# q and k of a fused encoder layer stored as high and low parts by their projections; stores of rows and memory tiles from GpSimd's queue; the memory tokens' splits issued step by step

## The chip, the cores and the metric

The kernel runs on one core of a Trainium2 chip. Its time is the device time of one execution in microseconds; three runs of the kernel before took 1416.4, 1417.2 and 1421.53 us, the median is 1417.2 us. PE is the matrix engine, DVE (VectorE), ACT (ScalarE) and POOL (GpSimd) are the other three that compute, SP only issues transfers. Transfers can also be issued from GpSimd's instruction stream.

## The reference

One layer of a streaming encoder: 1024 tokens, 1024 channels, one batch, all in float32.

```python
h = rms_norm(x, mix_pre_g);  proj = h @ w_in          # 512 + 3*512 + 8 columns: u | q | k | v | f_logit
y_ssm = s5_mixer(u, ...)                              # 32 groups x 16 channels, 64 complex states, then GLU
y_fox = forgetting_attention(q, k, v, f_logit + b)    # 8 heads x 64, causal, bias cum[q] - cum[k]
x = x + rms_norm(concat(rms_norm(y_ssm), rms_norm(y_fox)) @ w_out)
h = rms_norm(x, xa_pre_g)
x = x + rms_norm(memory_cross_attention(h, rms_norm(mem), wq, wkv, wo))   # 4 heads, 256 memory tokens
h = rms_norm(x, ffn_pre_g)
x = x + rms_norm((silu(h @ w_gate) * (h @ w_up)) @ w_down)                # 2816 hidden columns
```

## The kernel before

**Splits.** Matmuls keep float32 accuracy by splitting operands: `split` (lines 113 to 120) lets ScalarE write a rounded high part (L114) and VectorE the low part, the difference (L116, or L118 where a gain is multiplied in). `mm3` (L123 to L125) then makes three products: high by high, high by low, low by high. `load_w` (L153 on) loads a weight tile of 512 KB (L159) into one of two buffers "raw", or into another buffer when `stage` is given, and splits it into one of three "whl" buffers.

**Buffers.** Tiles come from small pools and a new tile waits until the last use of the one before it in its buffer: "a" and "b" have 2 buffers of 4 KB per partition, "c" 3, "d" and "e" 1, "t2" (rows and small tiles that go out) 3, "slab" 16. PSUM has 4 banks "g" and two pairs "s" for scores.

**Order.** A scheduler of the language orders each engine's instructions by the order of the code and by priorities; `high_priority` raises one, `issue_after` (in `behind`) keeps instructions behind a named one. Each engine and each transfer queue then works in that order, and an instruction that waits holds up all behind it.

**The stages.** Up to about 222 us: the input projection. It makes u, then the tiles 4 to 7 of qk (k of two heads each), v's first half, the forget gate, the tiles 0 to 3 (q), and between these, by a fixed pace, the steps of `ssm` on VectorE (L616 to L619 and others; ACT L621 writes their result; SP L627 loads the tables T). `qk_tile` (L285) has PE work (`proj_tile`), one scaled evacuation by VectorE per half (L289) and one store of the tile to `qk_d` in DRAM, from GpSimd's queue (L293). Then `ssm_out` (L638, L639 on PE) together with v's second half. From 222 to about 480 us: forgetting attention, `fox`, head by head and query tile by query tile (64 steps). In each step PE makes the scores (L734, L735, the mask L737); VectorE adds the bias and finds the row's minimum of the negated scores (L741); ScalarE takes the exponential and its sum (L743); VectorE normalises (L748), or GpSimd for the tiles 1, 3 and 5 of the heads from 2 on (L746); two steps later PE transposes (L765), and L768 or L770 evacuates; every second step of an odd head PE multiplies by v (L779). `prepare` loads the next head's q and k by eight transfers of 128 KB, in two halves (L714, L715), and splits them: ScalarE the high parts (L718, L114), VectorE for heads 0 and 1 and GpSimd from head 2 on the low parts (L719, L116).

**The fillers.** Beside the attention, `paced` takes a step of the generator `fillers` per attention step: `glu`, the first rows of `out_ssm`, `mem_load` (the memory tokens multiplied by their norm, L967, and split, eight pieces), 16 times `mem_tile` (24 matmuls of 256 columns, the evacuation L979, the store to `kv_d` L980), the rest of `out_ssm` (evacuation L845, store to `t_d` L849, 16 of them), and the start of cross-attention. These stores go out on `stB`, which is SP's queue, as all the loads do. From 480 us on come the output projection (w_out_f, L1034), cross-attention and the feed-forward layer, which takes more than half of the time; no line of these is changed.

Of the kernel before, what the change touches and what calls it, by code (L numbers as in the profile page):

```python
# [34 lines left out]
MAGIC = 12582912.0  # L35
POOL_T = (1, 3, 5)
RATE = 1.02
# [16 lines left out]
def layer(ctx: ExitStack, tc: tile.TileContext, a, out):  # L54
# [94 lines left out]
    boost = 5000  # L149
    stA, stB, stC = pool, sp, pool  # L150

# [26 lines left out]

    qk_d = dram.tile([8, P, S], F32, name="qk_d")
    v_d = dram.tile([NT, P, 512], F32, name="v_d")  # L180
# [104 lines left out]
    def qk_tile(i, xH, xL, rb, ahead=False):  # L285
        o = tt("a")

        def evac(h, hs, ps):
            dve.scalar_tensor_tensor(out=by_chunk(o)[:, 4 * h:4 * h + 4], in0=ps.rearrange("p (j c) -> p j c", j=4),  # L289
                                     scalar=-0.125 if i < 4 else 1.0,  # L290
                                     in1=rb[0][:, hs].rearrange("p (j c) -> p j c", j=4), op0=ALU.mult, op1=ALU.mult)
        yield from proj_tile(load_w(a["w_f"][i], P), xH, xL, evac, ahead)
        stA.dma_start(out=qk_d[i], in_=o)  # L293

# [400 lines left out]


    def fox(yf):
        heads, units, pts = {}, {}, {}
        sv = const.tile([P, NT], F32, name="sv_f")

        def prepare(h):
            r0 = (h % 2) * 64
            qs = tt("a", [P, S], F32R)
            ka = slab([P, 2, S])
            ncb = tt("b")
            sp.dma_start(out=ncb, in_=nc_d[h:h + 1, :].broadcast_to([P, S]))
            heads[h] = (qs, ka, ncb)
            eng = dve if h < 2 else pool
            for hf in range(2):
                hs = slice(hf * 512, hf * 512 + 512)  # L710
                qk = tt("d" if h == 0 and hf else "e", [P, 2, 512])
                qd, kd = qk[:, 0], qk[:, 1]
                for rr in (0, 64):
                    sp.dma_start(out=qd[rr:rr + 64], in_=qk_d[h // 2, r0:r0 + 64, hs])  # L714
                    sp.dma_start(out=kd[rr:rr + 64], in_=qk_d[4 + h // 2, r0:r0 + 64, hs])  # L715
                yield
                with behind():
                    act.activation(out=qs[:, hs], in_=qd, func=AF.Copy)  # L718
                    eng.tensor_tensor(out=qs[64:128, hs], in0=qd[64:128], in1=qs[64:128, hs].bitcast(F32),  # L719
                                      op=ALU.subtract)  # L720
                    split(ka[:, 0, hs], ka[:, 1, hs], kd, lo_eng=eng)

        def behind():
            return tc.issue_after(last[-1].ins) if last else ExitStack()

        def scores(h, t):
            qs, ka, ncb = heads[h]
            ke = (t + 1) * P
            ps = s_ps([P, S])
            qt = qs[:, t * P:(t + 1) * P]  # L730
            for c0 in range(0, ke, 512):
                c1 = min(ke, c0 + 512)
                dg = c1 == ke
                pe.matmul(ps[:, c0:c1], qt, ka[:, 0, c0:c1], start=True, stop=False)  # L734
                pe.matmul(ps[:, c0:c1], qt, ka[:, 1, c0:c1], start=False, stop=not dg)  # L735
                if dg:
                    pe.matmul(ps[:, ke - P:ke], identb, maskb, start=False, stop=True)  # L737
            sc = tt("c")
            nlr = sm(3, "nlr")
            nm, l, rl = (nlr[:, i:i + 1] for i in range(3))  # L740
            dve.tensor_tensor_reduce(out=sc[:, :ke], in0=ps[:, :ke], in1=ncb[:, :ke], scale=1.0,  # L741
                                     scalar=3e38, op0=ALU.add, op1=ALU.min, accum_out=nm)
            last.append(act.activation(out=sc[:, :ke], in_=sc[:, :ke], func=AF.Exp, scale=-1.0, bias=nm, accum_out=l))  # L743
            dve.reciprocal(out=rl, in_=l)
            if t in POOL_T and h > 1:
                pool.tensor_tensor(out=sc[:, :ke], in0=sc[:, :ke], in1=rl.broadcast_to([P, ke]), op=ALU.mult)  # L746
            else:
                dve.tensor_scalar(out=sc[:, :ke], in0=sc[:, :ke], scalar1=rl, scalar2=None, op0=ALU.mult)  # L748
            units[h, t] = sc
# [53 lines left out]
        vs = {}  # L803
        drain(prepare(0))
        load_v(0)
        for n in range(-lag, len(seq) + 1):
            if n + lag < len(seq):
                h, t = seq[n + lag]
                scores(h, t)
                if t == 1 and h + 1 < NH:  # L810
                    nxt = prepare(h + 1)
                if t % 2 and h + 1 < NH:
                    step(nxt)
                if (h, t) == (3, 5):
# [12 lines left out]
    def out_ssm(ys):  # L827
        for cc in range(4):
            wh, wl = load_w(a["w_out_s"][cc], 256)
            for j0 in range(0, NT, 2):  # L830
# [128 lines left out]
    def mem_load(r, out):  # L959
# [3 lines left out]
        for k in range(0, KT, 4):  # L963
            m = raw([P, 4, 256])
            sp.dma_start(out=m, in_=a["memT"].rearrange("(k p) m -> p k m", p=P)[:, k:k + 4])
            for kk in range(4):
                dve.tensor_tensor(out=m[:, kk], in0=m[:, kk], in1=rb, op=ALU.mult)  # L967
                split(mh[:, k + kk], ml[:, k + kk], m[:, kk], g_mem[:, k + kk:k + kk + 1])
                if kk % 2:
                    yield  # L970
        out.extend((mh, ml))

    def mem_tile(i, mh, ml):
        wh, wl = load_w(a["wkv"][i], P)
        ps = g_ps([P, 256])
# [648 lines left out]
```

## Time and profile before

| what | value |
| --- | --- |
| median of three runs | 1417.2 us |
| lowest, highest run | 1416.4, 1421.53 us |
| the profiled execution's own time | 1418.95 us |
| its span in the profile | 1417.2 us |
| its mean granted clock of PE | 0.99 |
| transfers, mean rate | 163 GB/s |

The span is counted from the first to the last instruction. A row of a timeline gives start, duration, engine, line, operation, what it writes and reads, and in brackets the idle time of the engine before it with what ended it. "SPq" is SP's transfer queue; a row there gives when a transfer was issued, not when it landed. In a table of waits, the engine and line that waited come first, then the one that ended the wait. The granted clock is the share of full speed that the matrix engine was given.

### The profile page before, as it was taken

What the parts mean: (1) busy time and instruction counts of PE and PEld (TensorE: products, weight loads), DVE (VectorE), ACT (ScalarE), POOL (GpSimd) and SP (SyncE); (2) the same over time, 40 slices, a digit from 0 to 9 for tenths busy, and PEclk for the clock granted to TensorE, in tenths of its full rate; (3) what the DMA queues carried; (4) which work ended last, traced back from release to release, by engine and by line L of the source; (5) the groups of instructions that cost most, each with busy time, mean ns of one, the idle gap of its engine ahead of it and who ended that gap; (6) DMA issues with size and microseconds to landing.
All of it is one profiled execution on the core that took longest, in us unless ns stands there. A gap on an engine that the chain in (4) does not pass through costs nothing.

```text
span 1417.2 us, 20364 instructions
## 1 busy us (share of the span) xinstructions
PE 1382.1 (98%) x7353; PEld 1162.5 (82%) x7353; DVE 948.5 (67%) x1693; ACT 658.7 (46%) x1305; POOL 403.2 (28%) x424
## 2 busy tenths in 40 slices
PE   9999999899899898999999999999999999999997
PEld 7889898689789686888888888888888888888886
DVE  8939937946566677636457677777776676555566
ACT  7372347866566555434334533333333334544441
POOL 0001000113243134002021467676666661000021
PEclk9999999899999999999999999999999999999999
DMA  6225554246543756024457255554444546955544
GB/s 216 91 90 136 156 179 130 75 148 188 182 129 103 198 178 220 15 75 148 164 179 266 98 186 186 185 186 149 149 156 156 171 149 234 346 207 191 180 163 164
DMA packets 109366, 231.07 MB, mean 163 GB/s; under 512 B 11720, under 2 KB 46536, under 8 KB 109136
## 3 DMA queue, kind: packets, MB, share of 16 engines
q1 hardware_dynamic: 94064, 178.34, 39.4%
q0 software_dynamic: 15200, 51.42, 10.2%
q8 instruction: 58, 0.95, 0.3%
q14 instruction: 44, 0.36, 0.1%
HBM read 165.23 MB, written 73.14 MB: 168 GB/s over the span
## 4 chain that ended last, share of the span: by engine, by line
PE 59%; DVE 1%; ACT 0%; issue 0%; DVEq 0%; ACTq 0%
PE x L1289 17%; PE g L1289 13%; PE x L1552 7%; PE g L1552 7%; PE x L125 2%; PE x L124 2%; PE x L123 2%; PE g L123 2%; PE g L125 2%; PE g L124 2%; PE g L1074 1%; PE g L1185 1%; DVE slab L116 0%; DVE whl L116 0%; DVE c L1062 0%
## 5 line engine op out<-in xcount | busy, mean ns | idle before, releaser
L1289 PE MATMUL x<-slab,op 128*128 128x512 f32 x984 | 233.2, 389 | 0.5 <-DVE op L116 0.5
L1289 PEld LDWEIGHTS x<-slab,op 128*128 128x128 f32 x984 | 184.6, 188 | 39.3 <-DVE op L116 1.0
L1289 PE MATMUL g<-slab,op 128*128 128x512 f32 x744 | 178.7, 389 | 0.0
L116 DVE TENSOR_TENSOR slab<-slab 128x1024 fp32r<-128x1024 f32 (+2 forms) x92 | 110.3, 1207 | 86.7 <-ACT slab L114 84.8
L1289 PEld LDWEIGHTS g<-slab,op 128*128 128x128 f32 x744 | 139.6, 188 | 29.0
L123 PE MATMUL g<-slab,whl 128*128 128x512 f32 (+1 forms) x416 | 151.7, 365 | 1.1 <-ACT t L979 0.7
L125 PE MATMUL g<-slab,whl 128*128 128x512 f32 (+1 forms) x416 | 148.7, 358 | 0.0
L124 PE MATMUL g<-slab,whl 128*128 128x512 f32 (+1 forms) x416 | 148.4, 357 | 0.0
L114 ACT ACTIVATE slab<-slab 128x1024 fp32r<-128x1024 f32 (+2 forms) x92 | 94.9, 1037 | 106.3 <-DMA slab<-hs_d 82.7
L1552 PE MATMUL g<-slab 128*128 128x512 f32 x462 | 126.6, 389 | 0.0
L1552 PE MATMUL x<-slab 128*128 128x512 f32 x462 | 126.6, 389 | 0.0
L1552 PEld LDWEIGHTS x<-slab 128*128 128x128 f32 x462 | 86.7, 188 | 18.0
L1552 PEld LDWEIGHTS g<-slab 128*128 128x128 f32 x462 | 86.7, 188 | 18.0
L116 DVE TENSOR_TENSOR whl<-raw,whl 128x1024 fp32r<-128x1024 f32 (+2 forms) x61 | 71.1, 1168 | 36.7 <-ACT whl L114 36.5
L116 DVE TENSOR_TENSOR op<-slab,op 128x512 fp32r<-128x512 f32 x80 | 86.4, 1091 | 11.6 <-ACT op L114 11.4
L123 PE MATMUL g<-whl,slab 128*128 128x256 f32 (+2 forms) x288 | 86.1, 307 | 5.0 <-ACT t L845 3.4
L123 PEld LDWEIGHTS g<-slab,whl 128*128 128x128 f32 x416 | 78.6, 189 | 12.2 <-ACT t L979 0.9
L125 PEld LDWEIGHTS g<-slab,whl 128*128 128x128 f32 x416 | 78.4, 189 | 11.8 <-DVE whl L116 0.2
L1365 POOL TENSOR_TENSOR wt<-wt 128x256 f32<-128x256 f32 x88 | 81.8, 930 | 19.6 <-DMA wt<-in_w_down 16.1
L124 PEld LDWEIGHTS g<-slab,whl 128*128 128x128 f32 x416 | 78.6, 189 | 10.6
L114 ACT ACTIVATE op<-slab 128x512 fp32r<-128x512 f32 x80 | 50.0, 627 | 78.5 <-PE x L1289 36.8
L124 PE MATMUL g<-whl,slab 128*128 128x256 f32 (+2 forms) x288 | 85.7, 298 | 0.0
(389 smaller groups left out, 2930.7 us busy)
## 6 DMA issues: line engine op xcount, KB each, us to landing
hs_d<-ev POOLq DMA_DIRECT2D x77, 256.0 KB, 2.6
slab<-hs_d SPq DMA_DIRECT2D x35, 512.0 KB
wt<-in_w_down SPq DMA_DIRECT2D x44, 256.0 KB
wt_d<-wt POOLq DMA_DIRECT2D x22, 512.0 KB, 4.7
slab<-in_w_gate SPq DMA_DIRECT2D x20, 512.0 KB
slab<-in_w_up SPq DMA_DIRECT2D x20, 512.0 KB
slab<-wt_d SPq DMA_DIRECT2D x20, 512.0 KB
wd_d<-in_w_down SPq DMA_DIRECT2D x33, 256.0 KB
```

The lines of the kernel that those rows point to most:

```text
L114: first = act.activation(out=hi, in_=src, func=AF.Copy, scale=1.0 if mul is None else mul)
L116: (lo_eng or dve).tensor_tensor(out=lo, in0=src, in1=hi.bitcast(F32), op=ALU.subtract)
L123: pe.matmul(ps, lh, rh, start=first, stop=False)
L124: pe.matmul(ps, lh, rl, start=False, stop=False)
L125: pe.matmul(ps, ll, rh, start=False, stop=last)
L1074: pe.transpose(tp[:, k], src[:, (k0 + k) * P:(k0 + k + 1) * P], ident)
L1185: turned = pe.transpose(tp[:, k], h3[:, (4 * n + k) * P:(4 * n + k + 1) * P], ident)
L1289: pe.matmul(ps, x[:, k], y[:, k], start=first and k + n == 0, stop=k == 3 and n == 2, skip_group_check=not first)
L1365: pool.tensor_tensor(out=o, in0=x, in1=y, op=ALU.subtract)
L1552: pe.matmul(banks[n][j], xo[:, u, js], wo[:, v], start=ends[0] and k == 0, stop=ends[1] and k == 2, skip_group_check=onto is not None)
```

## The change

1. `qk_d` gets a second plane. `qk_tile` splits each half of its tile as soon as that is evacuated (the high part into a "t2" tile, the low part in place) and stores the high halves and then the low tile from GpSimd's queue. The input projection has 16 splits of 128x512 more, and 24 stores instead of 8.
2. `prepare` loads q (high parts in the first 64 partitions, low parts in the others) and k (both parts, twice) straight into the tiles that PE reads: four transfers of 256 or 512 KB instead of eight of 128 KB. No engine splits a head any more: ScalarE loses 32 operations, VectorE and GpSimd the subtractions beside them.
3. All normalisations are VectorE's (18 leave GpSimd).
4. `stB` is GpSimd's queue: the 32 stores of rows and memory tiles leave SP's.
5. In `mem_load`, multiply and split of a piece are issued behind the latest exponential.
6. Every third memory tile's weights, and the third set of w_out_s, are loaded into the "e" buffer, which the heads no longer use.

```diff
-POOL_T = (1, 3, 5)
-    stA, stB, stC = pool, sp, pool
+    stA, stB, stC = pool, pool, pool
-    qk_d = dram.tile([8, P, S], F32, name="qk_d")
+    qk_d = dram.tile([8, 2, P, S], F32, name="qk_d")
 def qk_tile(i, xH, xL, rb, ahead=False):
-        o = tt("a")
+        hl = tt("a", [P, S], F32R)
+        o = hl.bitcast(F32)
...
-        stA.dma_start(out=qk_d[i], in_=o)
+        for h in range(2):
+            hs = slice(h * 512, h * 512 + 512)
+            hi = t2t([P, 512], F32R)
+            split(hi, hl[:, hs], o[:, hs])
+            stA.dma_start(out=qk_d[i, 0, :, hs], in_=hi.bitcast(F32))
+        stA.dma_start(out=qk_d[i, 1], in_=o)
 def prepare(h):
-            eng = dve if h < 2 else pool
-            for hf in range(2):
...
-                    sp.dma_start(out=qd[rr:rr + 64], in_=qk_d[h // 2, r0:r0 + 64, hs])
-                    sp.dma_start(out=kd[rr:rr + 64], in_=qk_d[4 + h // 2, r0:r0 + 64, hs])
-                yield
-                with behind():
-                    act.activation(out=qs[:, hs], in_=qd, func=AF.Copy)
-                    eng.tensor_tensor(out=qs[64:128, hs], in0=qd[64:128], in1=qs[64:128, hs].bitcast(F32),
-                                      op=ALU.subtract)
-                    split(ka[:, 0, hs], ka[:, 1, hs], kd, lo_eng=eng)
+            q, k = qs.bitcast(F32), ka.bitcast(F32)
+            for t in range(2):
+                sp.dma_start(out=q[t * 64:t * 64 + 64], in_=qk_d[h // 2, t, r0:r0 + 64])
+            for rr in (0, 64):
+                sp.dma_start(out=k[rr:rr + 64], in_=qk_d[4 + h // 2, :, r0:r0 + 64].rearrange("t p s -> p t s"))
 def scores(h, t):
-            if t in POOL_T and h > 1:
-                pool.tensor_tensor(out=sc[:, :ke], in0=sc[:, :ke], in1=rl.broadcast_to([P, ke]), op=ALU.mult)
-            else:
-                dve.tensor_scalar(out=sc[:, :ke], in0=sc[:, :ke], scalar1=rl, scalar2=None, op0=ALU.mult)
+            dve.tensor_scalar(out=sc[:, :ke], in0=sc[:, :ke], scalar1=rl, scalar2=None, op0=ALU.mult)
 def out_ssm(ys):
-            wh, wl = load_w(a["w_out_s"][cc], 256)
+            wh, wl = load_w(a["w_out_s"][cc], 256, stage="e" if cc == 2 else None)
 def mem_load(r, out):
-                dve.tensor_tensor(out=m[:, kk], in0=m[:, kk], in1=rb, op=ALU.mult)
-                split(mh[:, k + kk], ml[:, k + kk], m[:, kk], g_mem[:, k + kk:k + kk + 1])
+                with behind():
+                    dve.tensor_tensor(out=m[:, kk], in0=m[:, kk], in1=rb, op=ALU.mult)
+                    split(mh[:, k + kk], ml[:, k + kk], m[:, kk], g_mem[:, k + kk:k + kk + 1])
 def mem_tile(i, mh, ml):
-        wh, wl = load_w(a["wkv"][i], P)
+        wh, wl = load_w(a["wkv"][i], P, stage="e" if i % 3 == 2 else None)
```

The change moves instructions, and some lines of the file move with it: in the new file the lines of `split` are L113 (ScalarE) and L115 or L117 (VectorE), the S5 steps L616 to L619 are L621 to L624, the statistic L741 is L737, the head loads are L718 (q) and L720 (k), L748 is L741 and L967 is L959. The first place is VectorE in the input projection, around the third of four operations L619. Before:

```order
L616 TENSOR_TENSOR b<-c 128x896
L617 TENSOR_TENSOR b<-c 128x896
L618 TENSOR_TENSOR b<-b 128x896
L289 SCALAR_TENSOR_TENSOR a<-g,d 128x4x128
L619 TENSOR_TENSOR b<-b,slab 128x896
L616 TENSOR_TENSOR b<-c 128x896
L116 TENSOR_TENSOR whl<-raw,whl 128x1024
L617 TENSOR_TENSOR b<-c 128x896
```

And now, with the third L624 near the end:

```order
L621 TENSOR_TENSOR b<-c 128x896
L289 SCALAR_TENSOR_TENSOR a<-g,d 128x4x128
L622 TENSOR_TENSOR b<-c 128x896
L115 TENSOR_TENSOR whl<-raw,whl 128x1024
L623 TENSOR_TENSOR b<-b 128x896
L115 TENSOR_TENSOR a<-a,t_1868 128x512
L115 TENSOR_TENSOR a<-a,t_1872 128x512
L624 TENSOR_TENSOR b<-b,slab 128x896
L621 TENSOR_TENSOR b<-c 128x896
L289 SCALAR_TENSOR_TENSOR a<-g,d 128x4x128
```

A weight split and two subtractions of a k or q tile ("a" out of "a" and a t2 tile) stand ahead of that operation where none stood before; six more such subtractions stand further ahead. The second place is VectorE around the memory multiplies ("raw" out of "raw" and a t2 tile), with the statistic of 768 columns ("ISA c,nlr") behind them. Before:

```order
L677 TENSOR_TENSOR t_2672<-slab 128x512
L967 TENSOR_TENSOR raw<-raw,t_2736 128x256 x3
L678 SCALAR_TENSOR_TENSOR t_2672<-t_2671,t_2672 128x512
L967 TENSOR_TENSOR raw<-raw,t_2736 128x256 x5
L741 ISA c,nlr<-s,b 128x768
L741 ISA nlr 128x1
L118 SCALAR_TENSOR_TENSOR slab<-raw,gains,slab 128x256 x3
L118 SCALAR_TENSOR_TENSOR slab<-t_2672,gains,slab 128x512
L684 TENSOR_TENSOR d<-d,t_2671 128x512
L118 SCALAR_TENSOR_TENSOR slab<-raw,gains,slab 128x256
L118 SCALAR_TENSOR_TENSOR slab<-g,gains,slab 128x256
L118 SCALAR_TENSOR_TENSOR slab<-raw,gains,slab 128x256 x4
```

And now:

```order
L740 RECIPROCAL nlr<-nlr 128x1
L959 TENSOR_TENSOR raw<-raw,t_2762 128x256 x3
L683 SCALAR_TENSOR_TENSOR t_2707<-t_2706,t_2707 128x512
L741 TENSOR_SCALAR c<-c,nlr 128x640
L959 TENSOR_TENSOR raw<-raw,t_2762 128x256 x5
L737 ISA c,nlr<-s,b 128x768
L737 ISA nlr 128x1
L117 SCALAR_TENSOR_TENSOR slab<-raw,gains,slab 128x256 x2
L117 SCALAR_TENSOR_TENSOR slab<-t_2707,gains,slab 128x512
L689 TENSOR_TENSOR d<-d,t_2706 128x512
L117 SCALAR_TENSOR_TENSOR slab<-g,gains,slab 128x256
L740 RECIPROCAL nlr<-nlr 128x1
```

The multiplies still stand as three and five ahead of the statistic; behind it, of eight splits ("slab" out of "raw") four now come in two pairs, and the other four stand further on. The third place is SP's queue where the 16 memory tiles end and the loads of w_out_s begin. Before:

```order
L980 DMA kv_d<-t_3700 128x256
L159 DMA raw<-in_w_out_s 128x1024
L714 DMA e<-qk_d 64x512
L715 DMA e<-qk_d 64x512
L714 DMA e<-qk_d 64x512
L797 DMA slab<-v_d 128x8x256
L980 DMA kv_d<-t_3768 128x256
L715 DMA e<-qk_d 64x512
L159 DMA raw<-in_w_out_s 128x1024
L706 DMA b<-nc_d 128x1024
L980 DMA kv_d<-t_3822 128x256
L159 DMA raw<-in_w_out_s 128x1024
```

And now:

```order
L720 DMA slab<-qk_d 64x2x1024 x2
L158 DMA raw<-in_wkv 128x1024 x2
L158 DMA e<-in_wkv 128x1024
L158 DMA raw<-in_wkv 128x1024
L158 DMA raw<-in_w_out_s 128x1024
L158 DMA e<-in_w_out_s 128x1024
L158 DMA raw<-in_w_out_s 128x1024
L790 DMA slab<-v_d 128x8x256
L718 DMA a<-qk_d 64x1024 x2
L158 DMA raw<-in_wqT 128x1024
```

The stores to kv_d are gone from this queue, and the w_out_s loads stand together ahead of the load of v and of the head loads.

More of the change, by code (lines that the diff above doesn't have):

```diff
@@ L694, in glu_stats, with behind @@
         rsqrt_mean(r_s, sv, 512, 4 * EPS)
+    def behind():
+        return tc.issue_after(last[-1].ins)
     def fox(yf):
@@ L707, in prepare @@
             heads[h] = (qs, ka, ncb)
-            eng = dve if h < 2 else pool
-            for hf in range(2):
[L710 to L714, printed above, removed]
-                    sp.dma_start(out=kd[rr:rr + 64], in_=qk_d[4 + h // 2, r0:r0 + 64, hs])
-                yield
-                with behind():
-                    act.activation(out=qs[:, hs], in_=qd, func=AF.Copy)
-                    eng.tensor_tensor(out=qs[64:128, hs], in0=qd[64:128], in1=qs[64:128, hs].bitcast(F32),
-                                      op=ALU.subtract)
-                    split(ka[:, 0, hs], ka[:, 1, hs], kd, lo_eng=eng)
-        def behind():
-            return tc.issue_after(last[-1].ins) if last else ExitStack()
+            q, k = qs.bitcast(F32), ka.bitcast(F32)
[3 more added lines that the diff above has]
+                sp.dma_start(out=k[rr:rr + 64], in_=qk_d[4 + h // 2, :, r0:r0 + 64].rearrange("t p s -> p t s"))
         def scores(h, t):
@@ L803, in fox @@
         vs = {}
-        drain(prepare(0))
+        prepare(0)
         load_v(0)
@@ L810, in fox @@
                 if t == 1 and h + 1 < NH:
-                    nxt = prepare(h + 1)
-                if t % 2 and h + 1 < NH:
-                    step(nxt)
+                    prepare(h + 1)
                 if (h, t) == (3, 5):
```

## The prediction

> **What bounds the kernel now.** I read the page first, then the table of PE's waits, then windows of 35 and of 4 us, then the timelines around the four longest waits. The page's row of busy times:
>
> ```profile
> PE 1382.1 (98%) x7353; PEld 1162.5 (82%) x7353; DVE 948.5 (67%) x1693; ACT 658.7 (46%) x1305; POOL 403.2 (28%) x424
> ```
>
> PE is busy for 1382.1 of 1417.2 us, so 35.1 us are all its idle time. The change adds no matmul and drops none. It can only take PE's waits, and stretches of low granted clock, or add to them. These are the waits that matter, in the table of PE's waits (us in total, times, longest), and windows that hold three of them (busy us of PE, PEld, DVE, ACT, POOL with counts, granted clock, DMA share, GB/s):
>
> ```profile
> PE g L779 <- ACT t L979: 4.0, 1, 4.0
> PE g L123 <- ACT t L845: 3.4, 2, 2.4
> PE x L123 <- ACT slab L114: 3.2, 1, 3.2
> PE s L734 <- DVE nlr L741: 3.0, 1, 3.0
> ```
> ```profile
> 248.00:284.00 36.00, 29.82 (x169) 25.06 (x167) 34.40 (x72) 29.47 (x63) 6.10 (x4) 0.86 0.27 79
> 272.00:276.00 4.00, 3.11 (x13) 2.32 (x12) 4.00 (x12) 3.77 (x10) 1.17 (x1) 0.50 0.32 82
> 368.00:372.00 4.00, 2.83 (x16) 1.70 (x18) 1.39 (x2) 2.45 (x6) 0.61 (x1) 0.70 0.46 91
> 412.00:416.00 4.00, 1.61 (x15) 1.48 (x14) 1.44 (x4) 2.68 (x5) 1.84 (x2) 1.00 0.14 44
> ```
>
> After the waits of 3.0 and 4.0 us the granted clock falls (0.50 and 0.70), after the one of 2.4 us it stays at 1.00. So a wait of 3 us costs more than itself.
>
> **A, up to 284 us.** In the first window PE is idle for 36 − 29.82 = 6.2 us, and the lowered clock takes 0.14 × 29.82 = 4.2 us of full-speed work: 10.4 us in all. VectorE is full (34.40 of 36). Its timeline and PE's:
>
> ```profile
> 261.40 1.26 DVE L678 SCALAR_TENSOR_TENSOR t<-t,t 128x512 f32<-128x512 f32 x1
> 263.16 0.56 DVE L748 TENSOR_SCALAR c<-c,nlr 128x640 f32<-128x640 f32 x1
> 264.89 1.78 DVE L677 TENSOR_TENSOR t<-slab 128x512 f32<-128x512 f32 x1
> 266.60 1.08 DVE L967 TENSOR_TENSOR raw<-raw,t 128x256 f32<-128x256 f32 x3
> 267.60 0.68 DVE L678 SCALAR_TENSOR_TENSOR t<-t,t 128x512 f32<-128x512 f32 x1
> 268.20 1.75 DVE L967 TENSOR_TENSOR raw<-raw,t 128x256 f32<-128x256 f32 x5
> 269.88 0.94 DVE L741 CUSTOM_DVE_ANT_0 c<-s,b 128x768 f32<-128x768 f32 x1
> ```
> ```profile
> 270.89 0.79 PE L734 MATMUL s<-slab,a 128*128 128x512 f32 x1 [3.01 <-DVE nlr L741]
> 282.54 0.39 PE L123 MATMUL g<-whl,slab 128*128 128x256 f32 x1 [0.98 <-ACT t L845]
> ```
>
> PE waits for the statistic (L741) of 768 columns, behind five of the eight memory multiplies (L967). The new code means to spread these, but in the new order the same three and the same five still stand ahead of that statistic; only the splits behind it are parted, two by two. What goes is GpSimd's part of the head conversions, beside which VectorE's operations stretch: L678 took 1.26 us at 261.40 and 0.68 at 267.60, L677, of the same size, 1.78. Without that, 0.58 + 1.1 us, and with some 0.7 us of order, the statistic ends at about 268.4 instead of 270.8. PE's wait there shrinks only from 3.01 to about 1.9 us, since PE comes to it sooner too. Next in the chain is the first load of w_kv, which needs the fourth memory split:
>
> ```profile
> 273.71 2.31 SPq L159 DMA_DIRECT2D raw<-in_wkv  x2
> 277.53 1.06 ACT L114 ACTIVATE whl<-raw 128x1024 fp32r<-128x1024 f32 x1 [1.16 <-DMA raw<-in_wkv]
> ```
>
> In the new order that split ends at about 272.3 instead of 273.7: 272.3 + 3.8 (issue to use, 273.71 to 277.53) = 276.1, then ScalarE's 1.06, the same steps to the row evacuations as before, and PE goes on with its rows at 279.3, 3.2 us before the 282.54 of the trace. Two waits of about 1.4 us appear meanwhile for work that now comes too early, and with them the clock may fall as it did. So I take a gain of 2 us, between a loss of 2 (the clock falls further) and a gain of 10 (A goes).
>
> **C, 364 to 372 us.** ScalarE stood 5.76 us before a weight split, behind it the evacuation (L979) that PE needed:
>
> ```profile
> 358.26 1.70 SPq L159 DMA_DIRECT2D raw<-in_w_out_s  x1
> 367.79 1.06 ACT L114 ACTIVATE whl<-raw 128x1024 fp32r<-128x1024 f32 x1 [5.76 <-DMA raw<-in_w_out_s]
> ```
>
> The load took 9.5 us; it was issued behind a 1 MB load of v and a store that waited. In the new order all remaining w_out_s loads stand ahead of that v load and of the head loads around it, and the third has a buffer of its own ("e"). So the 4.0 us go, and with them 0.30·2.83 = 0.8 us of clock in this window and, by the same share, about as much behind it: 5.7 us. From below: 3 us, if another load comes late in its place.
>
> **D, 412 to 415 us.** ScalarE stood before a head conversion whose load was stuck behind stores on SP's queue:
>
> ```profile
> 398.09 7.09 SPq L849 DMA_DIRECT2D t_d<-t  x2
> 407.50 0.45 SPq L714 DMA_DIRECT2D e<-qk_d  x1
> 413.32 0.63 ACT L718 ACTIVATE a<-e 128x512 fp32r<-128x512 f32 x1 [3.14 <-DMA e<-qk_d]
> ```
>
> Both causes leave: the conversion is gone, and the stores are on GpSimd's queue. Gain 2.4 us (the second of the two waits on L845 in the table is A's 0.98). The window of 35 us after A, in which two heads are converted:
>
> ```profile
> 319.00:354.00 35.00, 34.29 (x276) 32.13 (x275) 24.02 (x45) 23.29 (x46) 11.97 (x10) 1.00 0.64 188
> ```
>
> Its 35 − 34.29 = 0.7 us of idle time are counted as gained too, from 0.
>
> **F, 480 us.** The 3.2 us of the table's third row wait for a load of w_out_f whose place on SP is behind head 7's last statistic, in the old order and in the new:
>
> ```profile
> 469.15 0.39 SPq L1034 DMA_DIRECT2D raw<-in_w_out_f  x1
> 482.30 1.06 ACT L114 ACTIVATE slab<-raw 128x1024 fp32r<-128x1024 f32 x1 [6.70 <-DMA raw<-in_w_out_f]
> ```
>
> I take 0, plus or minus 3, since what else moves in these 13 us shifts.
>
> **What the change adds: the input projection.** Sixteen splits of 128x512 move into a stretch where VectorE was full (columns as above):
>
> ```profile
> 142.00:177.00 35.00, 35.00 (x156) 28.96 (x155) 34.81 (x80) 12.60 (x18) 2.13 (x4) 1.00 0.54 155
> ```
> ```profile
> L116 DVE TENSOR_TENSOR slab<-e,slab 128x512 fp32r<-128x512 f32 x5 | 3.3, 687 | 0.1
> ```
> ```profile
> 175.93 1.09 DVE L619 TENSOR_TENSOR b<-b,slab 128x896 f32<-128x896 f32 x1
> 177.94 1.22 DVE L116 TENSOR_TENSOR whl<-raw,whl 128x1024 fp32r<-128x1024 f32 x1
> ```
> ```profile
> 177.05 0.97 SPq L627 DMA_DIRECT2D slab<-T_d  x2
> ```
> ```profile
> 185.74 0.39 PE L638 MATMUL g<-slab 128*128 128x128 f32 x2
> ```
>
> VectorE's 16 halves are 16 × 0.69 = 11.0 us; ScalarE's are as many, in a stretch where it is busy for 12.6 of 35 us, and cost nothing. Ahead of the third L619 now stand eight more subtractions and one weight split (1.22): 8 × 0.6 (0.69 less the 0.08 by which neighbours overlap, as at 266.60 and 267.60) + 1.15 = 5.95 us. The third L619 frees the slab into which T is loaded, so that load goes out at 183.0 instead of 177.05. With the 3.8 us of the w_kv load above it lands at 186.8, with a second load of 512 KB beside it at 188.4 or so; PE wants it at 185.74. The wait is 1.1 to 2.7 us; I take 2. Below it stands 0 (VectorE catches up in its gaps), above it 6, if a dip of the clock comes on top of 3 us and the last evacuations of the q tiles (L289) hold PSUM banks too.
>
> **The start of attention.** k of head 0 now lands in a slab that is free only after the last S5 matmul, and the first five score tiles stand one behind another on PE, where before other work lay between them:
>
> ```profile
> 213.63 0.39 PE L639 MATMUL g<-slab 128*128 128x128 f32 x2
> 226.08 0.34 PE L734 MATMUL s<-slab,a 128*128 128x384 f32 x1
> ```
> ```profile
> 227.21 0.54 DVE L741 CUSTOM_DVE_ANT_0 c<-s,b 128x384 f32<-128x384 f32 x1
> ```
>
> From 213.9 to the scores' new place, just ahead of 226, the 1 MB of k has 11 us, which is enough by the 3.8 us of half as much. But the fifth tile needs the statistic of the third, behind a weight split like that of 1.22 us above, and takes 0.54 us: waits of about 0.3, 0.1 and 1.2 us. I take 1.5 us, from 0 to 3.
>
> **Costs taken as nothing.** VectorE's 18 normalisations instead of GpSimd's: GpSimd took 1467 ns for 768 columns, VectorE 0.56 us for 640 (at 263.16), and in the fullest window from 284 to 461 us VectorE is busy for 24 of 35 us. If that cover is gone they cost at most 18 × 0.56 = 10 us. The 48 stores on GpSimd's queue hold up no matmul unless the three buffers (t2) that they empty run out. That window stands under D; GpSimd's group, and the page's list of DMA issues (KB each, median us to landing), are:
>
> ```profile
> L746 POOL TENSOR_TENSOR c<-c,nlr 128x768 f32<-128x768 f32 x6 | 8.8, 1467 | 18.2 <-DVE nlr L744 15.3 <-PE g L779 2.8
> ```
> ```profile
> qk_d<-a POOLq DMA_DIRECT2D x8, 512.0 KB, 4.0
> v_d<-t POOLq DMA_DIRECT2D x16, 128.0 KB, 3.3
> ```
>
> GpSimd's stores, those of the q and k tiles among them issued in windows like that of 34.81 us in 35, landed after 3.3 to 4.0 us. The 16 memory tiles run from the first load of w_kv (273.71) to the wait at 367.79: 94 / 16 = 5.9 us each, so one of three t2 buffers comes round after 17.6 us. The Trainium skill, SBUF — State Buffer, in the box 'The "DVE blocks DMA" trap (SWDGE)', speaks against this move: a DMA issued by GpSimd is held while VectorE runs a copy that takes both ports, since GpSimd can't then write its descriptors; in the next section its example lands after 3100 ns instead of 620. By that figure, an estimate, each store would land 2.5 us later, at some 6 us, within the 17.6, and the sum would not move. The rows of v_d and qk_d show no hold beyond their own 3.3 and 4.0 us.
>
> **The sum.** Gains 2 + 5.7 + 2.4 + 0.7 = 10.8 us; losses 2 + 1.5 = 3.5 us; net 7.3 us. The profiled execution took 1418.95 us, so 1411.65 by the sum; it lay 1.75 us over the median of the runs, 1417.2, so against the median I forecast 1409.9 us. By the terms' own ends, not all at once, this case reaches from about 1403 to 1416. A measurement of this kernel tells about 0.5%, 7.1 us, from no change, so the forecast lies on that bound.
>
> **The rivals.**
>
> 1. *More goes than I count.* A is one chain: with GpSimd off VectorE's back, the statistic may come early enough that no wait passes 3 us and the clock stays up. Then A gives 10.4 us and the two new waits of the start stay hidden: 10.4 + 5.7 + 2.4 + 0.7 = 19.2 us, 1398. For it: the stretched operations at 261.40 and 264.89. Against it: the five multiplies stay ahead of the statistic. Chance 0.15.
> 2. *The gain is given back.* The loads per head grow from 1.0 to 1.5 MB and are issued at once; some weight load that ScalarE waits for takes 9 us again, and C and D return elsewhere. Then 2 + 0.7 − 3.5 = −0.8 us: 1418. For it: the loads of 9.5 us at C and of 13 us at F. Against it: the weight loads stand ahead by a whole tile. Chance 0.20.
> 3. *The stores come late.* GpSimd's queue holds the memory and row stores until ScalarE finds no t2 buffer and PE no PSUM bank, from about 284 to 415 us. It decides from a landing of 17.6 us on; at 19.1 each round of three stores puts 1.5 us on PE, and 32 stores make 32 / 3 rounds: 16 us less the gain of 7.3 give 1426. For it: GpSimd's additions and its stores stand in one queue. Against it: landings of 3.3 to 4.0 us. Chance 0.07. The Trainium skill's rule (SBUF — State Buffer, the box named above) leads the same way, if the holds add up in the queue.
> 4. *VectorE bounds the input projection.* All 11.0 us of subtractions reach PE by way of T and the PSUM banks, with a dip of 1.7 us: 12.7 instead of 2, with the 1.5 of the start 14.2 against gains of 10.8, so 3.4 us slower than before, 1421; it outweighs the gains from 9.3 us on. For it: VectorE's 34.81 of 35 us. Against it: its results are used some time after they are ready. Chance 0.08, half of it beyond 0.5%, by longer dips.
>
> My forecast has 0.50. Of its reach from 1403 to 1416, 55% lie beyond 0.5% faster (1410.1).
>
> **How the numbers follow.** Faster: 0.55 × 0.50 + 0.15 = 0.43. Slower: 0.07 + 0.04 = 0.11. Same: 0.46. The range from 1397 to 1420 takes in the forecast's own 1403 to 1416, rival 2 and most of rivals 1 and 4.
>
> **What would show it.** Right, if in the profile after ScalarE has no wait for w_out_s or q/k loads between 350 and 420 us and PE's waits on L979's and L845's successors are gone, while a wait on the memory statistic of about 2 us and one of 1 to 3 us at the first S5 matmul (185 us) stand in PE's list. Wrong, if A's clock stays at 1.00 (rival 1), if a weight load still holds ScalarE for over 3 us (2), if ScalarE waits for stores of t_d or kv_d (3), or if PE idles by more than 6 us before 190 us (4). The stretch from 500 us to the end should keep its length.

## The result and the profile after

The changed kernel takes 1414.56 us (median of 19 runs, 1408.19 to 1418.33), the kernel before 1418.13 us in as many runs (1414.78 to 1422.74). The ratio is 0.997, with a 95% interval of 0.9959 to 0.9982: 3.6 us less, about half of the 7.3 us forecast, and under the half percent that the prediction counts as a change. Of all executions timed here one, of the kernel with the splits left out, ran slow (1530.09 us at a granted clock of 0.85), and its ratio below leaves it out. The profiled execution of the changed kernel, 1412.18 us with a span of 1410.4 us, is 6.8 us shorter than that of the kernel before, close to the forecast. So there are two things to explain: where the 6.8 us came from, term by term, and why the median shows only 3.6.

The table of PE's waits after the change (us in total, times, longest). The 4.0 us on L979 (L971 in the new file) and the 2.4 us on L845 (now L836) at 415 us are gone; the 2.2 us on L836 in the second row lie elsewhere, at A, where the kernel before had 0.40 and 0.98 us. The wait on the statistic is down to 2.0 us, the last row is new, and the row of w_out_f (ACT slab) has half its length:

```profile
PE s L730 <- DVE nlr L737: 3.5, 3, 2.0
PE g L758 <- ACT t L836: 2.2, 1, 2.2
...
PE x L122 <- ACT slab L113: 1.5, 1, 1.5
...
PE g L643 <- DMA slab<-T_d: 1.0, 1, 1.0
```

The windows in question (PE's busy time first, then PEld, DVE, ACT, POOL, the granted clock, DMA share, GB/s). In the first two PE idles 2.0 and 1.6 us, before 1.0 and 0.1. From 272 us on the clock falls, and it stays low for longer than before: 0.91 in the window from 284 us, before 1.00. From 354 to 425 us PE is never idle:

```profile
177.00:213.00 36.00, 34.01 (x257) 32.12 (x256) 16.92 (x20) 16.25 (x25) 5.37 (x10) 1.00 0.64 220
213.00:248.00 35.00, 33.43 (x225) 29.59 (x224) 19.02 (x43) 21.43 (x42) 2.16 (x4) 1.00 0.53 135
248.00:284.00 36.00, 32.24 (x184) 27.46 (x182) 28.81 (x71) 25.20 (x53) 0.00 (x0) 0.85 0.36 89
284.00:319.00 35.00, 34.29 (x269) 29.91 (x270) 18.53 (x41) 21.87 (x50) 3.63 (x6) 0.91 0.61 177
354.00:390.00 36.00, 36.00 (x295) 31.09 (x295) 22.43 (x51) 21.18 (x44) 6.01 (x9) 1.00 0.60 185
390.00:425.00 35.00, 35.00 (x290) 31.04 (x289) 22.10 (x60) 22.41 (x52) 6.89 (x9) 1.00 0.67 180
```

A ledger can be read from marks that both kernels have: the mask matmul of a score tile, taken where the order has the same matmuls ahead of it in both. Four rows of PE's timeline after the change, for the tiles (1,3), (2,3), (4,3) and (6,3):

```profile
260.13 0.23 PE L733 MATMUL s<-maskb,identb 128*128 128x128 bf16 x1
310.50 0.23 PE L733 MATMUL s<-maskb,identb 128*128 128x128 bf16 x1
374.12 0.23 PE L733 MATMUL s<-maskb,identb 128*128 128x128 bf16 x1
424.09 0.23 PE L733 MATMUL s<-maskb,identb 128*128 128x128 bf16 x1
```

| mark | before | after | after later by | what lies since the mark above |
| --- | --- | --- | --- | --- |
| first S5 matmul | 185.74 | 188.77 | +3.03 | input projection: +3.0 |
| tile (1,3) | 255.03 | 260.13 | +5.10 | start of attention: +2.1 |
| tile (2,3) | 305.72 | 310.50 | +4.78 | A: -0.3 |
| tile (3,6) | 351.78 | 355.49 | +3.71 | small wait at 335 us: -1.1 |
| tile (4,3) | 376.22 | 374.12 | -2.10 | C: -5.8 |
| tile (6,3) | 428.81 | 424.09 | -4.72 | D: -2.6 |
| first w_out_f matmul | 483.41 | 477.08 | -6.33 | F: -1.6 |
| end of the span | 1417.2 | 1410.4 | -6.8 | the rest: -0.5 |

### The profile page after: what moved, and what is told of

Its sections match the earlier page's. It is cut to its first block, busy times and chain, and to the rows that moved or that the text cites. A ratio compares the mean times of both kernels' runs of the same rounds, so it can differ in the third digit from the quotient of the medians.

```text
span 1410.4 us, 20272 instructions
## 1 busy us (share of the span) xinstructions
PE 1381.5 (98%) x7353; PEld 1163.3 (82%) x7353; DVE 952.1 (68%) x1719; ACT 652.8 (46%) x1289; POOL 378.7 (27%) x430
## 4 chain that ended last, share of the span: by engine, by line
PE 60%; DVE 1%; ACT 0%; issue 0%; DVEq 0%; ACTq 0%
PE x L1281 17%; PE g L1281 13%; PE x L1544 7%; PE g L1544 7%; PE x L123 2%; PE x L124 2%; PE g L122 2%; PE x L122 2%; PE g L124 2%; PE g L123 2%; PE g L1066 1%; PE g L1177 1%; DVE c L1054 0%; DVE whl L115 0%; ACT yt L1048 0%
## 5 line engine op out<-in xcount | busy, mean ns | idle before, releaser
L115 DVE TENSOR_TENSOR slab<-slab 128x1024 fp32r<-128x1024 f32 (+2 forms) x92 | 110.6, 1208 | 86.6 <-ACT slab L113 84.4
L113 ACT ACTIVATE slab<-slab 128x1024 fp32r<-128x1024 f32 (+2 forms) x92 | 94.9, 1036 | 107.9 <-DMA slab<-hs_d 79.0
L115 DVE TENSOR_TENSOR op<-slab,op 128x512 fp32r<-128x512 f32 x80 | 84.4, 1066 | 11.6 <-ACT op L113 11.3
L122 PE MATMUL g<-whl,slab 128*128 128x256 f32 (+2 forms) x288 | 86.8, 310 | 1.2 <-ACT yt L318 0.7
L123 PEld LDWEIGHTS g<-slab,whl 128*128 128x128 f32 x416 | 78.6, 189 | 10.8
L113 ACT ACTIVATE op<-slab 128x512 fp32r<-128x512 f32 x80 | 50.0, 627 | 79.3 <-PE x L1281 38.0
L124 PE MATMUL g<-whl,slab 128*128 128x256 f32 (+2 forms) x288 | 85.9, 299 | 0.0
L123 PE MATMUL g<-whl,slab 128*128 128x256 f32 (+2 forms) x288 | 85.9, 298 | 0.0
```

The source lines that it names most:

```text
L113: first = act.activation(out=hi, in_=src, func=AF.Copy, scale=1.0 if mul is None else mul)
L115: (lo_eng or dve).tensor_tensor(out=lo, in0=src, in1=hi.bitcast(F32), op=ALU.subtract)
L122: pe.matmul(ps, lh, rh, start=first, stop=False)
L123: pe.matmul(ps, lh, rl, start=False, stop=False)
L124: pe.matmul(ps, ll, rh, start=False, stop=last)
```

## The experiments

Each was made from the changed kernel unless it says otherwise, and is given as a ratio to the kernel before, timed on the same chip.

**Splits left out.** In `qk_tile`:

```diff
-            hi = t2t([P, 512], F32R)
-            split(hi, hl[:, hs], o[:, hs])
-            stA.dma_start(out=qk_d[i, 0, :, hs], in_=hi.bitcast(F32))
+            stA.dma_start(out=qk_d[i, 0, :, hs], in_=o[:, hs])
```

> The changed kernel, but the projections store each q and k tile unsplit into both planes, so 16 high parts on ScalarE and 16 subtractions on VectorE are left out and the attention's scores are computed from q and k taken twice. Theory (the splits in the full stretch of VectorE cost PE time): the wait for T at the first S5 matmul (0.96 us) goes, score tile (1,0), 5.1 us later in the changed kernel than in the kernel before, comes 2 to 5 us earlier, and the time falls by as much, to 0.993 to 0.996 of the kernel before. Rival (the lateness comes from the later k load and the order of PE's work, the splits are hidden): the lateness stays over 4 us and the time stays at 0.997.

Measured: 1411.29 us, 0.9939 [0.9919, 0.9960]. The load of T goes out 7.1 us earlier than the 182.94 us of the changed kernel, PE's window from 177 us is that of the kernel before, and tile (1,3) comes 2.9 us earlier:

```profile
175.88 0.82 SPq L630 DMA_DIRECT2D slab<-T_d  x2
```
```profile
257.25 0.23 PE L731 MATMUL s<-maskb,identb 128*128 128x128 bf16 x1
```

So the splits cost 2.9 of the 5.1 us. The rest, the start of attention, stays when they are gone. That it belongs to the new place of k's load and of the score tiles is argued; no run puts these back.

**The stores' queue, from both sides.** First the stores back on SP's queue, then the kernel before with nothing but its stores on GpSimd's:

```diff
-    stA, stB, stC = pool, pool, pool
+    stA, stB, stC = pool, sp, pool
```

> The changed kernel, with the stores of rows and memory tiles back on SP's queue. Theory (the gain at 368 and 413 us comes from the conversions that left ScalarE and from loads issued ahead; the stores' queue matters little): loads of w_kv and of the heads go out later, some PE waits of 1 to 3 us return, 0.997 to 1.000 of the kernel before. Rival (stores on GpSimd's queue land late or hold t2 buffers, and so take back part of the gain): faster than the changed kernel, under 0.996.

Measured: 1413.13 us, 0.9966 [0.9949, 0.9983], no different from the changed kernel. No wait of PE returns between 290 and 460 us, where the theory had some of 1 to 3 us.

```diff
-    stA, stB, stC = pool, sp, pool
+    stA, stB, stC = pool, pool, pool
```

> The kernel before, with one part of the change alone: the stores of rows and memory tiles on GpSimd's queue. Theory (the waits at 369 and 415 us come from conversions on ScalarE whose loads stood behind these stores on SP's queue): the wait of 2.4 us on L845 goes, the one of 4.0 us on L979 at least in part, and nothing is added in the input projection: 4 to 8 us less, 0.994 to 0.997. Rival (only the removal of the conversions takes these waits; with them gone the stores' queue made no difference): both waits stay over 2 us, 0.999 to 1.000.

Measured: 1419.22 us, 1.0006 [0.9992, 1.0020]. The rival holds on the time and for C: ScalarE still stands before a split of w_out_s and before a head conversion, and PE's 4.0 us on L979 are 3.4. At D PE's 2.4 us became 1.4 us on another evacuation, and by the marks that stretch is 0.5 us shorter than before, of the 2.6 us that the whole change takes:

```profile
369.28 1.06 ACT L114 ACTIVATE whl<-raw 128x1024 fp32r<-128x1024 f32 x1 [5.14 <-DMA raw<-in_w_out_s]
415.66 0.63 ACT L718 ACTIVATE a<-e 128x512 fp32r<-128x512 f32 x1 [2.98 <-DMA e<-qk_d]
```
```profile
PE g L779 <- ACT t L979: 3.4, 1, 3.4
```

Neither taking the stores off SP's queue alone nor putting them back matters much. What takes C and D, then? Their stretches, tile (3,6) to (4,3) and (4,3) to (6,3), take 24.4 and 52.6 us before and 18.6 and 50.0 after. They are as short as that in each kernel that takes one other part of the change back: the splits, the stores' queue, and below the e buffer, `behind` and the normalisations. That leaves the second part, heads that arrive split, unless two of the others stand in for each other; it was not run alone. Within it, D is the conversion, before which ScalarE still waits 2.98 us when the stores are off the queue. C is another case: ScalarE waited there for weights of w_out_s, and not for a conversion. In the new order a load of these goes out ahead of the load of v (358.03 against 361.30 us), and ScalarE waits for none of them. That this order is what takes C is argued and not shown.

**The e buffer.** `stage=None` for w_kv and w_out_s:

> The changed kernel, with all weights of memory tiles and w_out_s in the two raw buffers, none in the e buffer. Theory (the weight loads' lead keeps ScalarE from waiting): ScalarE waits for w_kv or w_out_s by 1 to 4 us somewhere from 290 to 380 us, and PE behind it: 1 to 4 us slower than the changed kernel, 0.998 to 1.000. Rival (the two buffers are enough, once no stores and conversions stand between the loads): within 1 us of 0.997.

Measured: 1414.77 us, 0.9981 [0.9969, 0.9993]. ScalarE's waits are there, up to 4.08 us on w_kv, but PE waits only 0.87 us behind the longest of them. By the marks that costs 1.1 us from (2,3) to (3,6), which is the gain of the small wait at 335 us; the median can't be told from the changed kernel's.

```profile
343.61 1.06 ACT L113 ACTIVATE whl<-raw 128x1024 fp32r<-128x1024 f32 x1 [4.08 <-DMA raw<-in_wkv]
```
```profile
344.99 0.38 PE L122 MATMUL g<-slab,whl 128*128 128x256 f32 x1 [0.87 <-ACT t L971]
```

**A: load or multiplies?** The changed kernel at A, on PE, on SP's queue and on ScalarE. PE's wait on the statistic is followed by slower matmuls (0.63 instead of 0.40 us for 512 columns, at a clock of 0.61 from 272 to 276 us). The load of w_kv is issued right behind one of q and takes 5.6 us. The evacuation of rows (L836) stands behind its split on ScalarE, and PE waits 2.21 us for that:

```profile
273.33 0.80 PE L730 MATMUL s<-slab,a 128*128 128x512 f32 x1 [2.00 <-DVE nlr L737]
273.93 0.63 PE L731 MATMUL s<-slab,a 128*128 128x512 f32 x1
```
```profile
275.44 1.11 SPq L718 DMA_DIRECT2D a<-qk_d  x2
276.64 8.24 SPq L158 DMA_DIRECT2D raw<-in_wkv  x2
```
```profile
282.21 1.06 ACT L113 ACTIVATE whl<-raw 128x1024 fp32r<-128x1024 f32 x1 [2.95 <-DMA raw<-in_wkv]
284.20 0.82 ACT L836 ACTIVATE t<-g,r_s 128x256 f32<-128x256 f32 x2
```
```profile
284.71 0.47 PE L758 MATMUL g<-ident,c 128*128 128x128 f32 x1 [2.21 <-ACT t L836]
```

The clock (third figure from the end) in the window around that wait, first in the kernel before, then in the changed one:

```profile
284.00:288.00 4.00, 4.00 (x37) 3.22 (x37) 1.62 (x6) 2.95 (x9) 0.00 (x0) 1.00 0.72 220
```
```profile
284.00:288.00 4.00, 3.29 (x15) 2.89 (x17) 3.24 (x8) 4.00 (x12) 0.72 (x1) 0.50 0.57 184
```

Which of the two decides? The first kernel gets the first weights early, the second moves the multiplies:

```diff
-        wh, wl = load_w(a["wkv"][i], P, stage="e" if i % 3 == 2 else None)
+        wh, wl = load_w(a["wkv"][i], P, stage="e" if i % 3 == 0 else None)
```

> The changed kernel, with the e buffer given to memory tiles 0, 3, 6 and so on instead of 2, 5, 8, so that the first tile's weights are loaded long before the memory splits. Theory (what holds the place at 270 to 290 us is the first load of w_kv, on which ScalarE waits 2.95 us and behind it the row evacuations): that wait and PE's 2.21 us go, and with them part of the low clock: 2 to 5 us less, 0.994 to 0.996. Rival (the wait on the statistic and the clock after it set that place): PE's 2.00 us and the clock of 0.5 stay and the time changes by less than 1 us.

Measured: 1413.91 us, 0.9964 [0.9949, 0.9979], no gain. ScalarE's wait for the first weights is gone, and so is PE's on the statistic, which now stands ahead of the multiplies. But another result stands behind them instead, the sum of squares d, and PE waits longer than before:

```profile
273.79 1.75 DVE L959 TENSOR_TENSOR raw<-raw,t 128x256 f32<-128x256 f32 x5
...
278.29 0.68 DVE L689 TENSOR_TENSOR d<-d,t 128x512 f32<-128x512 f32 x1
```
```profile
279.03 1.87 PE L237 MATMUL g<-ones,d 128*128 128x1 f32 x8 [5.20 <-DVE d L689]
```

```diff
-                    dve.tensor_tensor(out=m[:, kk], in0=m[:, kk], in1=rb, op=ALU.mult)
+                    pool.tensor_tensor(out=m[:, kk], in0=m[:, kk], in1=rb, op=ALU.mult)
```

> The changed kernel, with the eight memory multiplies on GpSimd instead of VectorE. Theory (the load of w_kv decides): PE's wait on the statistic of 768 columns, 2.00 us, goes, but the resumption behind the w_kv load comes no earlier, perhaps later since GpSimd is slower: from 2 us less to 1 us more. Rival (the statistic decides, by its wait and the clock that falls after it): the clock stays over 0.9 from 272 to 290 us and 4 to 6 us go, 0.993 to 0.995.

Measured: 1410.68 us, 0.9939 [0.9918, 0.9961], and by the score tiles 17.1 us from (1,6) to (2,1) instead of 22.0. (That stretch takes 20.1 to 23.0 us in the profiles of the other kernels with the multiplies on VectorE.) PE's wait on the statistic is 0.36 us. Of the 4.9 us, 1.0 is idle time of PE and 3.9 the clock. The time speaks against my theory, that the load decides, but the two kernels don't settle it: the first has a longer wait in place of the one that it takes away, and in the second the row evacuations also stand ahead of the w_kv split on ScalarE, so that PE's 2.21 us go as well:

```profile
280.71 0.84 ACT L836 ACTIVATE t<-g,r_s 128x256 f32<-128x256 f32 x2
...
283.27 1.06 ACT L113 ACTIVATE whl<-raw 128x1024 fp32r<-128x1024 f32 x1 [0.71 <-DMA raw<-in_wkv]
```

The rival is right on the time, not on its sign: the clock still falls, though for less long (0.94, 0.50 and 0.71 in the three windows from 272 us; 0.61, 0.50, 0.50 and 0.50 in four in the changed kernel). GpSimd's eight multiplies take 7.51 us, and VectorE's operations beside them stretch, L683 from 0.69 to 1.20 us:

```profile
268.65 7.51 POOL L959 TENSOR_TENSOR raw<-raw,t 128x256 f32<-128x256 f32 x8 [38.39 <-ACT t L175]
```
```profile
268.73 1.20 DVE L683 SCALAR_TENSOR_TENSOR t<-t,t 128x512 f32<-128x512 f32 x1
```

**The change's own step for A undone.** `mem_load` without `with behind()`:

> The changed kernel, with the memory multiplies and splits not kept behind an exponential, as in the kernel before. Theory (that part moves four splits and none of the multiplies that hold the statistic): the wait on the statistic stays at about 2 us and the time within 1 us of the changed kernel, 0.996 to 0.998. Rival (the parted splits let the first load of w_kv out earlier and save time): 1 to 3 us slower, 0.998 to 1.000.

Measured: 1414.35 us, 0.9965 [0.9953, 0.9978], wait on the statistic 2.0 us. The theory holds: that part does nothing here that the runs can tell.

**The normalisations back on GpSimd** (tiles 1, 3 and 5 from head 2 on):

> The changed kernel, with the normalisations of tiles 1, 3 and 5 of the heads from 2 on back on GpSimd. Theory (they are off the path on either engine): within 1 us of the changed kernel, 0.996 to 0.998. Rival (on GpSimd they stretch VectorE's operations and delay the stores behind them): 2 us slower or more, 0.998 to 1.000.

Measured: 1413.19 us, 0.9955 [0.9937, 0.9973]. That is 1.4 us under the changed kernel, where the theory had 1 us either way, and within the intervals: not slower, and no gain of the choice of engine that these runs can tell.

**The spread.** The load of w_out_f behind F took 11.5 us in the profile after and 13.1 in that before, and 11.0 to 13.8 in the experiments other than the two below, from the same place in SP's order. Is it the spread? Held loads of x, alone and with the multiplies on GpSimd:

```diff
         xt = tt("c")
+        if n < 2:
+            dve.tensor_copy(xt[:, 0:1], wo[1][:, 1, 0:1].bitcast(F32))
         sp.dma_start(out=xt, in_=a["x"][ts, :])
```

> The changed kernel, with the first two loads of x for the output projection held until the second part of w_out_f has been split (VectorE writes one element of the target from that part first), so that 1 MB less shares the transfers with that load. Theory (the load of w_out_f at 464 us takes 11 to 14 us by chance of the transfers, and the matrix engine's wait on it and the clock after it make most of the spread between executions of a kernel): the load takes under 11 us, PE's wait is under 1 us, the clock stays at 1.00 from 476 to 488 us; the median falls by 2 to 4 us, 0.994 to 0.996, and the runs spread by less than the 10 us of the changed kernel. Rival (the spread is elsewhere): median at 0.997, spread as before.

Measured: 1414.55 us, 0.9970 [0.9957, 0.9983], runs from 1409.86 to 1417.38. In its profile the load takes 10.8 us, PE's wait is 0.89 us and the clock is 1.00 from 476 to 488 us, all as the theory has it, and the median still doesn't move.

> The changed kernel, with the held loads of x and with the memory multiplies on GpSimd. Theory (two places, independent): the gains add, 3 to 4 us of the multiplies and 2 to 4 us of the loads: 0.990 to 0.993. Rival (what one frees the other takes): no better than the multiplies alone, 0.994.

Measured: 1411.09 us, 0.9949 [0.9935, 0.9964], that is, no better than the multiplies alone. The load took 12.4 us here (second row; the first is that of the kernel above):

```profile
474.91 1.06 ACT L113 ACTIVATE slab<-raw 128x1024 fp32r<-128x1024 f32 x1 [4.38 <-DMA raw<-in_w_out_f]
```
```profile
472.65 1.06 ACT L113 ACTIVATE slab<-raw 128x1024 fp32r<-128x1024 f32 x1 [6.00 <-DMA raw<-in_w_out_f]
```

So holding the loads of x doesn't keep it short, and where it was short the time was no less: F is not most of the spread. The theory fell. What differs between executions shows in a second profile of the changed kernel:

> The changed kernel itself, a second profile. Theory (executions differ by the transfers before the waits at 189 and 477 us and by where the clock falls, not in the work): score tiles and waits agree within 0.1 us but for those of T (0.96 us) and w_out_f (1.55 us), which are longer, and the span is 1 to 4 us over the 1410.4 us of the first profile. Rival (the difference is spread over the whole span, or lies in the feed-forward layer): the stretch from 490 us to the end differs by more than 1.5 us.

Measured: span 1412.5 us, 2.1 over the first. The wait for T is 1.50 us and that for w_out_f 2.41, as expected. But score tile (1,3) is 2.1 us later, of which 1.5 come from the clock at the start of attention, and A is 1.1 us shorter, with a clock of 0.93 instead of 0.50 from 284 to 288 us. At the start of attention PE waited 0.57 and 0.90 us in both executions, but in the second the clock fell (first pair of windows: first profile; second pair: second profile):

```profile
230.00:234.00 4.00, 3.10 (x17) 2.25 (x18) 3.64 (x13) 2.10 (x8) 0.13 (x1) 1.00 1.03 271
234.00:238.00 4.00, 4.00 (x20) 3.27 (x19) 2.68 (x8) 2.63 (x7) 0.00 (x0) 1.00 0.51 168
```
```profile
230.00:234.00 4.00, 2.57 (x11) 1.82 (x11) 3.64 (x14) 2.44 (x7) 0.54 (x1) 0.85 1.01 248
234.00:238.00 4.00, 4.00 (x16) 3.24 (x17) 1.99 (x6) 1.09 (x3) 0.00 (x0) 0.72 0.64 213
```

**The subtractions of the q and k tiles on GpSimd as well as the multiplies** (`lo_eng=pool` in `qk_tile`'s split):

> The changed kernel, with the memory multiplies on GpSimd, and the 16 subtractions of the q and k tiles there too instead of on VectorE. Theory (VectorE's extra 11 us delay the load of T; GpSimd is idle for most of that stretch): the load of T goes out before 180 us, PE's wait for it goes, score tile (1,0) comes 2 to 3 us earlier than in the changed kernel, and the time is 2 to 3 us under that of the multiplies alone: 0.991 to 0.993. Rival (a VectorE operation with two inputs in SBUF stretches beside one of GpSimd by as much as GpSimd takes off it): VectorE stays full, T comes no earlier, and the time is that of the multiplies alone or more, 0.994 to 0.996.

Measured: 1428.68 us, 1.0065 [1.0044, 1.0086], 18 us slower than with the multiplies alone: neither the theory nor the rival. VectorE had no gap from 108 to 131 us, and one subtraction on GpSimd took 13.09 us there; the next, with VectorE idle, took 1.27. The t2 tiles and the stores of v stood behind it, ScalarE waited 14.56 us for a buffer and PE 9.0 us for ScalarE:

```profile
118.98 13.09 POOL L115 TENSOR_TENSOR a<-a,t 128x512 fp32r<-128x512 f32 x1 [12.54 <-ACT t L113]
132.02 0.57 POOL L297 DMA_DIRECT2D qk_d<-t  x1
132.62 1.27 POOL L115 TENSOR_TENSOR a<-a,t 128x512 fp32r<-128x512 f32 x1
```
```profile
134.48 0.47 ACT L316 ACTIVATE t<-g,r_x 128x256 f32<-128x256 f32 x1 [14.56 <-DMA qk_d<-t]
```
```profile
137.19 0.59 PE L122 MATMUL g<-whl,slab 128*128 128x264 f32 x1 [9.01 <-ACT yt L318]
```

## Why the prediction was right, and where not

**C and D** (5.7 and 2.4 us forecast): 5.8 and 2.6, and the same in the second profile. Right in size. Of the causes that I gave for D, the conversion counts and the stores' queue hardly does, as the two kernels on that queue show. Of those that I gave for C, the third buffer ("e") isn't needed; that the w_out_s loads stand ahead fits the traces, and no run tests it alone.

**The small wait** near 335 us: 1.1 us, 0.7 forecast. It comes back when the e buffer isn't used.

**The input projection** (2 us): the load of T went out at 182.94 us, where I had 183.0, and the wait was 0.96 us in the first profile and 1.50 in the second, where I had 1.1 to 2.7. That working holds. The term came out at 3.0, 1 us over the forecast: T took 5.8 us from issue to use, where I had 3.8 to 5.4 and took a value between. The wait is only a part of the 3.0, since PE came to it 1.9 us late, by work whose cost I had put at nothing. The hi tiles take t2 buffers that v's evacuations need, and ScalarE waits for their stores:

```profile
122.19 0.48 ACT L316 ACTIVATE t<-g,r_x 128x256 f32<-128x256 f32 x1 [3.60 <-DMA qk_d<-t]
```
```profile
127.29 0.39 PE L122 MATMUL g<-whl,slab 128*128 128x264 f32 x1 [0.67 <-ACT yt L318]
```

That is 0.7 of the 1.9 us. Another 0.7 come at 102.76 us, where an evacuation (L485) stands behind two of the high parts that I had ScalarE do for nothing, and PE waits 0.43 us; the other 0.5 lie near 81 us, beside three high parts. I had named t2 for the memory tiles and the rows, not for the place where the change adds its users. But these 1.9 us don't add to the 3.0: had PE come earlier, it would have waited for T by that much more, since VectorE, which frees T's slab, had no gap from 120 to 170 us. This is worked out and not tested. The kernel without splits gets back 2.9 us, all but 0.1 of the 3.0.

**The start of attention** (1.5 us, of waits of 0.3, 0.1 and 1.2): 2.1 us, with waits of 0.57 and 0.90 that the profile names; 0.6 lie in no wait of PE. In the second profile it is 3.6, by the clock.

**A** (a gain of 2 us): 0.3 in the first profile, 1.5 in the second. The wait on the statistic was 2.00 us where I had 1.9. The first load of w_kv took 5.6 us instead of the 3.8 that I took over; that the load of q just ahead of it is the reason is argued. PE goes on with its rows at 285.07 us, 2.6 us earlier than before if counted from tile (1,3), where I had 3.2. What undid the gain is the clock behind that point: I had left open that it falls as it did, but it stayed at 0.50 from 284 to 288 us, where it had been at 1.00. In the second profile it was 0.93 there, and 1.1 us more of the gain remain. Moving the multiplies wins 4.9 us, most of it clock, without telling apart the statistic and the row evacuations.

**F** (0, plus or minus 3): -1.6 in this pair of profiles, by a load that took 11.5 us. In the profiles of its variants PE waited there from 0.9 to 3.9 us, 2.4 in the second profile of the changed kernel itself, and 2.8 and 3.2 with the old order. So I don't count it as a gain of the change.

**The sum.** By these terms the two profiles differ by 6.8 us, 7.3 forecast. That is close in part by luck: the input projection, the start and A cost 3.3 us more than forecast, C, D and the small wait gave 0.7 more, and F and the rest, for which I had put nothing, gave 2.1. The step that failed is the comparison: I set the sum of one profiled execution against the median of three runs as if both kernels' profiles lay equally far from their medians. They lie 0.8 us over the median (1418.95 to 1418.13) and 2.4 us under it (1412.18 to 1414.56), which is the difference of 6.8 and 3.6 us. The second profile, at 1414.23 us, is nearer to the median. By the same marks it has +3.7 and +3.6 up to tile (1,3), then -1.5 (A), -1.1, -5.8 (C), -2.6 (D), -0.7 (F) and -0.3, together -4.7: C, D and the small wait repeat, the other terms differ by up to 1.5 us between two executions of one kernel.

Of the rivals, the second (the gain given back) is nearest in time, but not by its mechanism: C and D did not return. The third did not come: the stores of t_d and kv_d landed after 3.3 and 2.1 us (medians), far from 17.6. The fourth is seen in small: 3.0 us by way of T, where it had 12.7 with the PSUM banks. The kernel with the multiplies on GpSimd, at 1410.68 us, is nearest to the time that I had forecast, by a step that isn't in the change.

## What to carry to other kernels

Where an engine's in-order stream made others wait, it helped here to take instructions out of the stream (the head conversions, the memory multiplies); clearing the queue of the stores, or loading the first w_kv weights earlier, did not. New users of a small rotating buffer are to be costed where they are added, not only where the buffer was tight before. A loss ahead of a later wait costs nothing of its own if that wait ends no later for it. A single profile differs from its kernel's median by up to 3 us here, so a gain below that is judged from many runs, and its terms from marks that have the same work ahead of them.

## What the runs showed of the hardware

In one place a GpSimd subtraction with both inputs in SBUF took 13.09 us, against 1.27 for the next one with VectorE idle. VectorE ran operations with two inputs all that time without a gap, and the subtraction ended 1.1 us after the last of them (130.95 and 132.07 us). The Trainium skill, SBUF — State Buffer, section "Who interferes with whom", says that a VectorE instruction with two inputs in SBUF and a GpSimd instruction that reads SBUF exclude each other, the second to issue waiting until the first is done. These rows agree on the exclusion, and go further than one instruction: GpSimd did not get in between VectorE's back-to-back operations. That isn't always so. The eight memory multiplies on GpSimd ended within 7.51 us beside a VectorE that was as full, from 268 to 275 us, and there VectorE's 128x512 operations took 1.20 us (L683) instead of 0.69. What decides which of the two gives way stays open.

The granted clock is not decided by the length of one wait: it fell after waits of 2.00 us in both profiles of the changed kernel, stayed up after 2.39 us in the kernel before, and after the same waits of 0.57 and 0.90 us it fell in one execution and not in the other. I had drawn the line at about 3 us. The Trainium skill, TensorE: Matmul & The Clock Gate, Part 1, has a free-running window of some 3.4 us that is checked for activity; a free-running window would explain that the same waits end differently, which is argued and not shown. Of 19 runs of the changed kernel, the fastest (1408.19 us) had a mean granted clock of 0.995, the slowest (1418.33 us) 0.988; the correlation of clock and time over all is -0.75. What starts a fall in a given execution stays open.
